# A two-layer hybrid encoder on one core: the order of the instructions on TensorE, VectorE and ScalarE, written out anew

## The chip, the core and the metric

The kernel runs on one core of a Trainium2 chip. The metric is device time in microseconds (us) for one execution. Work goes to five engines, each with its own instruction row that it runs strictly from front to back: TensorE (PE in the profile; PEld is its loading of the stationary operand), VectorE (DVE), ScalarE (ACT), GpSimd (POOL) and SyncE (SP), which issues the weight DMAs here. Engines wait for each other by semaphores. An instruction that waits holds up everything behind it in its own row.

## What is computed

Two layers on a sequence of 256 tokens of width 1024. Cut to what matters:

```python
for i in range(2):
    proj = x @ w_in[i]                       # 1024 -> 13824, split into ten parts
    y_a = multiscale_pool(a_in) @ w_branch_a[i]
    y_b = dilated_attention(q, k, v) @ w_branch_b[i]      # 12 heads, three dilations
    y_c = hgrn2_bidirectional(q_h, i_h, f_fwd, f_bwd, g_h) @ w_branch_c[i]   # 8 heads
    merged = gates[0] * y_a + gates[1] * y_b + gates[2] * y_c
    x1 = layer_norm(ALPHA * x + merged @ w_out[i])
    hidden = silu(x1 @ w_ffn_gate[i]) * (x1 @ w_ffn_up[i])
    ple = (p[i] @ w_ple_proj[i]) * sigmoid(x1 @ w_ple_gate[i])
    x = layer_norm(ALPHA * x1 + hidden @ w_ffn_down[i] + ple)
```

All is float32. The recurrence of branch C is computed without a loop over tokens: running products of the forget gate (scans) and their reciprocals turn it into small matrix products per block of 64 tokens.

## The kernel before

**Chunks.** All weights stream through as chunks of 1 MB (`raw`, by SyncE, L197), three buffers deep. A chunk is split into two reduced-precision parts: ScalarE copies it to `whi` (L210), VectorE subtracts to get `wlo` (L211). TensorE then makes three products per tile (L252 to L254: hi by hi, hi by lo, lo by hi); the FFN's first half uses two wider ones (L272). A chunk is 48 products with 256 moving columns or 24 with 512. Activations are split alike, into `xx`.

```python
PE.matmul(ps, lhsT=ah, rhs=bh, start=first, stop=False)    # L252
PE.matmul(ps, lhsT=ah, rhs=bl, start=False, stop=False)    # L253
PE.matmul(ps, lhsT=al, rhs=bh, start=False, stop=last)     # L254
```

**A layer in order.** V of branch C (4 chunks), its output gate (4), then four head pairs, each with three chunks (query, forward and backward forget gate) and, for the first three, two chunks of the attention's V; twelve chunks of attention queries and keys; four of pooling; the three branches with their gates; the output projection and norm 1; the per-layer embedding (`pl2`); 22 chunks of FFN gate and up; 11 of FFN down and norm 2.

**Background tasks.** What branch C, attention and pooling do between their chunks are Python generators (`hgrn_task`, `attn_task`, `pool_task`). After each chunk `step_end` splits the next chunk and then runs `background`, which resumes a task until about 3000 estimated ns are handed out. A `yield None` puts a task to sleep until the next chunk. For a head pair and direction, `hgrn_task` puts on VectorE: two scans (L388/L390 or L393/L396), two reciprocals (L401, L403), four products (L405 to L409), one copy, eight small products (L431, L433), one tiny product (L437) and two more (L441). On TensorE follow 8 block products (L451) and, after the second direction, 8 more (L461) and 4 (L468); later the products with V (L492, L493) and transposes (L517). Attention's transposes are L553.

**The norms.** `rows_gemm` fills four PSUM banks (two token halves t, two column halves) and holds the last two or three chunks, so that the half t=0 is complete first. `layer_norm` then adds the residual (L341/L343), takes statistics (L344 to L348), has GpSimd raise to the power -0.5 (L320), corrects that on VectorE (L322 to L325), scales in two steps (L353, L355), and TensorE transposes the result (L330) so that the next stage can use it (split by L311 and L312).

**What sets the order.** Only the opening stretch (first chunks and transposes of `x`) runs in the order in which it is written. After that the programming layer's scheduler places the instructions on each engine by its own estimates.

Of the kernel before, what the change touches and what calls it, by code (L numbers as in the profile page):

```python
# [15 lines left out]
P = 128  # L16
# [62 lines left out]
def trunk(ctx: ExitStack, tc: tile.TileContext, x, p, w_in, pool_w, pool_scale, w_branch_a,  # L79
# [4 lines left out]

    cst = ctx.enter_context(tc.tile_pool(name="cst", bufs=1))
# [36 lines left out]
    def load_x(t):  # L122
        for hf in range(2):
            cs = slice(512 * hf, 512 * hf + 512)
            nc.sync.dma_start(out=xt[:, t, cs], in_=x[0, t * P:(t + 1) * P, cs])
# [13 lines left out]
    for l in range(DEPTH):  # L139
        for c0 in (C_IH, C_IH + 512, C_GH, C_GH + 512):  # L140
            blk(w_in[l], 0, c0)
            blk(w_in[l], 512, c0)
        for hp in range(4):
            for c0 in (C_QH, C_FF, C_FB):
                cols(w_in[l], c0 + 256 * hp)
            if hp < 3:
                blk(w_in[l], 0, C_VA + 512 * hp)
                blk(w_in[l], 512, C_VA + 512 * hp)
# [37 lines left out]
    def pieces(i, k):  # L186
        n = {0: 4, 1: 2}.get(i, 1)
        return [slice(j * k // n, (j + 1) * k // n) for j in range(n)]

    def dma_chunk():  # L190
        i = pos["dma"]
        if i >= NCH:
            return
        src, k = chunks[i]
        t = wp.tile([P, k, 2048 // k], F32, tag="raw", name="raw")
        for ks in pieces(i, k):
            nc.sync.dma_start(out=t[:, ks, :], in_=src[:, ks, :])  # L197
        raw[i] = t
        pos["dma"] += 1

    def split_chunk():
        i = pos["split"]
        if i >= NCH:
            return
        k = chunks[i][1]
        t = raw.pop(i)
        hi = wp.tile([P, k, 2048 // k], F32R, tag="whi", name="whi")
        lo = wp.tile([P, k, 2048 // k], F32R, tag="wlo", name="wlo")
        for ks in pieces(i, k):
            A.activation(out=hi[:, ks, :], in_=t[:, ks, :], func=AF.Copy)  # L210
            V.tensor_tensor(out=lo[:, ks, :], in0=t[:, ks, :], in1=f(hi[:, ks, :]), op=ALU.subtract)  # L211
        split[i] = (hi, lo)
        pos["split"] += 1
        dma_chunk()
# [6 lines left out]

    tasks = []
    busy = []

    def background(budget=3000, width=3):
        slept = set()
        while budget > 0:
            act = [t for t in tasks[:width] if id(t) not in slept]
            if not act:
                return  # L230
            t = act[0]
            try:
                c = next(t[1])
                if c is None:
                    slept.add(id(t))
                else:
                    budget -= c
            except StopIteration:
                tasks.remove(t)

    def finish(kind):
        while any(t[0] == kind for t in tasks):
            background(10 ** 9)

    def step_end():
        split_chunk()
        background()
# [8 lines left out]
    def gemm_cols(w, act, ps, nk=8, m0=0, nm=2):  # L256
        for m in range(nm):
            for k in range(nk):
# [31 lines left out]
    def gemm_tok(ws, act, evac, between):  # L290

        nk = 4 * len(ws)
        for t in range(2):
            ps = gbank()
            for k in range(nk):
                w = ws[k // 4]
                mm3(ps, act(k, t), (w[0][:, k % 4, :], w[1][:, k % 4, :]), k == 0, k == nk - 1)
                if t == 0 and k == 5 and between is not None:
                    between()
            evac(t, ps)  # L300

    def tok_block(act, evac, between=None, n=2):
        ws = [use_chunk() for _ in range(n)]
        gemm_tok(ws, act, evac, between)
        for _ in range(n):
            step_end()
# [11 lines left out]
    def rsqrt(out, v, n):  # L318
        y = small([P, n], "rs_y")
        G.tensor_tensor(out=y, in0=v, in1=mhalf.to_broadcast([P, n]) if n > 1 else mhalf, op=ALU.pow)  # L320
# [6 lines left out]
    def transpose_x(t, hf):  # L327
        ps = tbank()
        for k in range(4):
            PE.transpose(ps[:, k * P:(k + 1) * P], xt[:, t, (4 * hf + k) * P:(4 * hf + k + 1) * P], ident)  # L330
        v = ps.rearrange("p (k t) -> p k t", t=P)
        split_to(xh[:, 4 * hf:4 * hf + 4, t * P:(t + 1) * P],
                 xl[:, 4 * hf:4 * hf + 4, t * P:(t + 1) * P], v)

    def layer_norm(t, gb, ress, then):

        st = small([P, 2, 6], "ln_st")
        for hf, (base, scale, ps) in enumerate(ress):
            dst = xt[:, t, 512 * hf:512 * hf + 512]
            if scale is None:  # L340
                V.tensor_tensor(out=dst, in0=base, in1=ps, op=ALU.add)  # L341
            else:
                V.scalar_tensor_tensor(out=dst, in0=base, scalar=scale, in1=ps, op0=ALU.mult, op1=ALU.add)  # L343
            V.bn_stats(out=st[:, hf, :], in_=dst)  # L344
        mv = small([P, 2], "ln_mv")
        V.bn_aggr(out=mv, in_=st)
        ve = small([P, 1], "ln_ve")
        V.tensor_scalar(out=ve, in0=mv[:, 1:2], scalar1=LN_EPS, scalar2=None, op0=ALU.add)  # L348
        r = small([P, 1], "ln_r")
        rsqrt(r, ve, 1)  # L350
        for hf in range(2):
            cs = slice(512 * hf, 512 * hf + 512)
            V.scalar_tensor_tensor(out=xt[:, t, cs], in0=xt[:, t, cs], scalar=mv[:, 0:1], in1=gb[:, 0, cs],  # L353
                                   op0=ALU.subtract, op1=ALU.mult)
            V.scalar_tensor_tensor(out=xt[:, t, cs], in0=xt[:, t, cs], scalar=r, in1=gb[:, 1, cs],  # L355
                                   op0=ALU.mult, op1=ALU.add)
            then(t, hf)
# [8 lines left out]
    def hgrn_task(l, hp, q, ff, kf, fb, kb, vt, gt, oh, ol):  # L366
# [14 lines left out]
        for d in range(2):  # L381
# [63 lines left out]
            if dg is None:  # L445
                dg = tbank()
            for h in range(2):
# [24 lines left out]
            yield None  # L472
# [11 lines left out]
        A.activation(out=al, in_=lg.rearrange("p (g c) -> p g c", c=P), func=AF.Copy)  # L484
        yield 660
        yield None
        po = tbank()
# [6 lines left out]
        yield None  # L494
# [7 lines left out]
        rsqrt(r, ms, 4)  # L502
        yield 700
        yield None
        for t in range(2):
# [5 lines left out]
            yield 400  # L511
        yield None
        pt = tbank()
# [4 lines left out]
        yield None  # L518
        for h in range(2):
# [3 lines left out]
            yield 330  # L523


    def attn_task(j, qs, ks, va, vb, ob):
        hh = j % 2
        sj = slope(j)
        po = None
        for t in range(2):  # L530
# [5 lines left out]
            yield None  # L536
# [7 lines left out]
            A.activation(out=sc, in_=sc, func=AF.Exp, bias=nm, accum_out=den)  # L544
            yield 900
            rd = small([P, 1], "rd")
            V.reciprocal(out=rd, in_=den)
            V.tensor_scalar(out=sc, in0=sc, scalar1=rd, scalar2=None, op0=ALU.mult)
            yield 500
            yield None  # L550
            pp = tbank()
# [4 lines left out]
            yield None  # L556
            if po is None:
                po = tbank()
            o = po[:, t * P:(t + 1) * P]
            js = slice(j * P, (j + 1) * P)  # L560
# [4 lines left out]
        yield None  # L565
# [5 lines left out]
        yield 330  # L571


    def pool_task(g, a, mix):

        while busy or any(t[0] == "attn1" for t in tasks):
            yield None
# [26 lines left out]
        yield 850  # L604
        mh, ml = half2k([P, 2, S], F32R), half2k([P, 2, S], F32R)
        split_to(mh, ml, a[:, :, 8:264])
        mix[g] = (mh, ml)
# [5 lines left out]
    load_x(0)  # L613
    dma_chunk()
    dma_chunk()
    load_x(1)
    dma_chunk()
    start = ctx.enter_context(ExitStack())
    start.enter_context(tc.manual_schedule(engines={
        mybir.EngineType.Activation, mybir.EngineType.DVE, mybir.EngineType.PE}))  # L620
    for hf in range(2):
        transpose_x(0, hf)
    split_chunk()
    split_chunk()
    def begin():
        for hf in range(2):
            transpose_x(1, hf)
        split_chunk()

# [35 lines left out]
    for l in range(DEPTH):  # L665
# [3 lines left out]
        for hf in range(2):  # L669
            def ev(t, ps):  # L670
                A.activation(out=vt[:, t, 512 * hf:512 * hf + 512], in_=ps, func=AF.Copy)
            tok_block(xtok, ev, begin if l == 0 and hf == 0 else None)
            if l == 0 and hf == 0:
                start.close()
            if l == 0 and hf == 1:
                load_constants()
        for hf in range(2):
            def ev(t, ps):
                s = misc([P, 512])
# [280 lines left out]
```

## Time and profile before

| | |
|---|---|
| median of 3 runs | 1318.82 us (1318.72 to 1318.83) |
| the profiled execution | 1319.02 us; from its first to its last instruction 1317.2 us |
| granted TensorE clock, mean | 0.997 |
| TensorE busy / weight load | 1292.2 us / 1140.0 us |
| VectorE / ScalarE / GpSimd busy | 900.2 / 617.4 / 20.0 us |
| moved by DMA | 233.36 MB, mean 177 GB/s |

Busy times of TensorE are unions of pipelined, overlapping instructions; what a product costs is read from the distance between the starts of two. In a row of the timeline stand the start, the duration, engine, line, operation, output<-inputs, shape, how many in a row, and in brackets how long the engine had been idle before and what released it. Lines are those of the kernel before (L252) unless the changed kernel is named.

### The profile page before, as it was taken

How to read it: one execution, taken by the hardware profiler on the slowest of the kernel's cores; microseconds unless marked ns; L12 is line 12 of the kernel's file. 1: busy time of each engine (PE TensorE's matmuls, PEld its weight loads, DVE VectorE, ACT ScalarE, POOL GpSimd, SP SyncE). 2: the span in 40 equal slices, each digit the busy share in tenths (PEclk: the TensorE clock that was granted, in tenths of full speed). 3: DMA queues.
4: the chain of work that ended last, by engine and by line, in shares of the span. 5: the costliest groups of instructions: out<-in, count | busy, mean ns of one | idle time of the engine just before them, and what ended most of it. 6: DMA issues, size and time to landing. Idle time of an engine off the chain costs nothing.

```text
span 1317.2 us, 18830 instructions
## 1 busy us (share of the span) xinstructions
PE 1292.2 (98%) x7881; PEld 1140.0 (87%) x7881; DVE 900.2 (68%) x1230; ACT 617.4 (47%) x732; POOL 20.0 (2%) x24
## 2 busy tenths in 40 slices
PE   8999999999999999999989999999999999999997
PEld 6899999998888788888779999999988887888885
DVE  4697998575656776664555989975846658666645
ACT  5444445444444455553344444445534444555531
POOL 0000000000000000000000000000000000000000
PEclk9999999999999999999999999999999999999999
DMA  8655444244656466655356545453355664766550
GB/s 301 206 183 170 160 160 161 97 158 157 197 199 223 161 224 192 191 188 197 128 176 208 169 152 170 152 181 107 128 192 192 198 226 140 243 192 189 187 197 34
DMA packets 160276, 233.36 MB, mean 177 GB/s; under 512 B 3840, under 2 KB 108864, under 8 KB 160192
## 3 DMA queue, kind: packets, MB, share of 16 engines
q1 hardware_dynamic: 158496, 227.44, 52.4%
q10 hardware_dynamic: 1696, 4.72, 1.1%
q8 instruction: 62, 1.02, 0.3%
q14 instruction: 22, 0.18, 0.0%
HBM read 231.10 MB, written 1.05 MB: 176 GB/s over the span
## 4 chain that ended last, share of the span: by engine, by line
PE 91%; DVE 6%; ACT 1%; issue 1%; POOL 1%; DMA 0%; POOLq 0%; SPq 0%; DVEq 0%; ACTq 0%
PE g L252 22%; PE g L253 22%; PE g L254 22%; PE t L272 9%; PE g L272 9%; DVE wlo L211 2%; ACT whi L210 1%; PE t L451 1%; POOL rs_y L320 1%; PE t L492 1%; PE t L493 1%; PE t L468 0%; PE t L330 0%; DVE ln_st L344 0%; PE t L533 0%
## 5 line engine op out<-in xcount | busy, mean ns | idle before, releaser
L211 DVE TENSOR_TENSOR wlo<-raw,whi 128x2048 fp32r<-128x2048 f32 (+2 forms) x218 | 490.1, 2249 | 305.7 <-ACT whi L210 305.3
L210 ACT ACTIVATE whi<-raw 128x2048 fp32r<-128x2048 f32 (+2 forms) x218 | 410.1, 1883 | 368.5 <-PE g L254 191.6
L252 PE MATMUL g<-xx,whi 128*128 128x256 f32 x896 | 256.9, 287 | 0.0
L253 PE MATMUL g<-xx,whi 128*128 128x256 f32 x896 | 253.9, 283 | 0.0
L254 PE MATMUL g<-xx,wlo 128*128 128x256 f32 x896 | 253.7, 283 | 0.0
L252 PE MATMUL g<-whi,xx 128*128 128x512 f32 x480 | 189.5, 395 | 1.7 <-ACT whi L210 1.6
L253 PE MATMUL g<-wlo,xx 128*128 128x512 f32 x480 | 189.2, 394 | 1.4 <-DVE wlo L211 1.4
L254 PE MATMUL g<-whi,xx 128*128 128x512 f32 x480 | 188.0, 393 | 0.0
L252 PEld LDWEIGHTS g<-xx,whi 128*128 128x128 f32 x896 | 171.7, 192 | 0.7
L253 PEld LDWEIGHTS g<-xx,whi 128*128 128x128 f32 x896 | 171.8, 192 | 0.2
L254 PEld LDWEIGHTS g<-xx,wlo 128*128 128x128 f32 x896 | 171.6, 192 | 0.0
L272 PE MATMUL t<-xx,whi 128*128 128x512 f32 x352 | 123.6, 396 | 0.0
L272 PE MATMUL g<-xx,whi 128*128 128x512 f32 x352 | 123.6, 396 | 0.0
L252 PEld LDWEIGHTS g<-whi,xx 128*128 128x128 f32 x480 | 91.6, 191 | 21.5 <-ACT whi L210 2.2
L253 PEld LDWEIGHTS g<-wlo,xx 128*128 128x128 f32 x480 | 91.6, 191 | 21.0 <-DVE wlo L211 2.6
L254 PEld LDWEIGHTS g<-whi,xx 128*128 128x128 f32 x480 | 91.3, 190 | 18.9
L272 PE MATMUL g<-xx,wlo 128*128 128x256 f32 x352 | 90.9, 279 | 0.0
L272 PE MATMUL t<-xx,wlo 128*128 128x256 f32 x352 | 90.9, 279 | 0.0
L253 PE MATMUL g<-wlo,s 128*128 128x512 f32 x224 | 87.5, 391 | 0.0
L254 PE MATMUL g<-whi,s 128*128 128x512 f32 x224 | 87.5, 390 | 0.0
L252 PE MATMUL g<-whi,s 128*128 128x512 f32 x224 | 87.1, 390 | 0.0
L272 PEld LDWEIGHTS g<-xx,whi 128*128 128x128 f32 x352 | 64.5, 188 | 12.0
(181 smaller groups left out, 1662.5 us busy)
## 6 DMA issues: line engine op xcount, KB each, us to landing
raw<-in_w_in_dram SPq DMA_DIRECT2D x106, 1024.0 KB, 5.1
raw<-in_w_ffn_gate_dram SPq DMA_DIRECT2D x22, 1024.0 KB, 5.3
raw<-in_w_ffn_up_dram SPq DMA_DIRECT2D x22, 1024.0 KB, 5.4
raw<-in_w_ffn_down_dram SPq DMA_DIRECT2D x22, 1024.0 KB, 4.9
raw<-in_w_branch_c_dram SPq DMA_DIRECT2D x8, 1024.0 KB, 5.1
raw<-in_w_branch_a_dram SPq DMA_DIRECT2D x8, 1024.0 KB, 5.0
raw<-in_w_out_dram SPq DMA_DIRECT2D x8, 1024.0 KB, 5.3
raw<-in_w_ple_gate_dram SPq DMA_DIRECT2D x8, 1024.0 KB, 5.1
```

Source lines behind the costliest of these rows:

```text
L210: A.activation(out=hi[:, ks, :], in_=t[:, ks, :], func=AF.Copy)
L211: V.tensor_tensor(out=lo[:, ks, :], in0=t[:, ks, :], in1=f(hi[:, ks, :]), op=ALU.subtract)
L252: PE.matmul(ps, lhsT=ah, rhs=bh, start=first, stop=False)
L253: PE.matmul(ps, lhsT=ah, rhs=bl, start=False, stop=False)
L254: PE.matmul(ps, lhsT=al, rhs=bh, start=False, stop=last)
L272: PE.matmul(o, lhsT=a, rhs=b, start=k == 0 and i == 0, stop=k == KD - 1 and i == 1, skip_group_check=True)
L320: G.tensor_tensor(out=y, in0=v, in1=mhalf.to_broadcast([P, n]) if n > 1 else mhalf, op=ALU.pow)
L451: PE.matmul(dg[po:po + 64, co:co + 64], lhsT=KI[:, cs], rhs=QI[:, cs], start=True, stop=True)
L492: PE.matmul(o, lhsT=at[:, 2 * h + t, :], rhs=vt[:, t, hs], start=True, stop=False)
L493: PE.matmul(o, lhsT=al[:, 2 * h + 1 - t, :], rhs=vt[:, 1 - t, hs], start=False, stop=True)
```

## The change

The whole kernel now keeps TensorE, VectorE and ScalarE in the order in which the code is written (`manual_schedule` at its start). The code is rewritten for that:

- `step_end` runs the background first, then a stage's evacuation, then the split of the next chunk. A new `amid` stands in the middle of each chunk's products and wakes sleeping tasks there, so that a task's TensorE part stands amid a chunk's products. `background` takes tasks in turn.
- Banks and 2 KB buffers are counted by hand (`banks_for`, `room`). Before a stage takes a buffer of which ten are held, `room` runs background tasks until one is free. Two head pairs' tasks hold ten.
- The output gate's four chunks (G) move from before the head pairs to behind the first pair's three; the attention's V follows one pair later. Pooling's weight chunk moves behind branch B.
- A norm becomes class `Norm` (`add`, `rest`) and the step after it class `Handover`: the half t=0 is normalised while TensorE finishes t=1; t=1's norm stands ahead of the splits of the next two chunks on VectorE (`split_later` gives their ScalarE half first); the next stage begins with products that need only t=0 and only `whi`.
- The head: `x` and the first two chunks are loaded and split in smaller pieces, in the order of their use, and four products on zeros (`spin`) run on TensorE before and after the first transposes.

The counts of products and other operations are the same but for the four `spin` products, one memset and some splits cut in pieces. In the diff, `go`'s arguments are the token half, the column half, the chunk and which of the three products; `a` and `b` of `Handover` are the two chunks still held. The diff, cut to its core:

```diff
+    ctx.enter_context(tc.manual_schedule(engines={
+        mybir.EngineType.Activation, mybir.EngineType.DVE, mybir.EngineType.PE}))
...
+    def amid(width=3):
+        for t in tasks[:width]:
+            if id(t) in asleep:
+                asleep.discard(id(t))
+                resume(t)
     def background(budget=3000, width=3):
-        slept = set()
+        turn = 0
         while budget > 0:
-            act = [t for t in tasks[:width] if id(t) not in slept]
+            act = [t for t in tasks[:width] if id(t) not in asleep]
             if not act:
                 return
-            t = act[0]
...
+            t = act[turn % len(act)]
+            turn += 1
+            budget -= resume(t) or 0
+    def room(n):
+        while held[0] + n > 10:
+            amid()
+            background(1000)
+        held[0] += n
-    def step_end():
-        split_chunk()
-        background()
+    def step_end(then=None):
+        background()
+        if then is not None:
+            then()
+        split_chunk()
...
     def gemm_cols(w, act, ps, nk=8, m0=0, nm=2):
         for m in range(nm):
+            if m == 1:
+                amid()
...
             for i in range(6):
                 ps = gbank()
                 gemm_cols(use_chunk(), xk, ps)
+                room(1)
                 t = half2k([P, 512])
...
+        class Handover:
+            def __init__(self, norms, banks, part, a, b):
+                norms[0].rest()
+                part(*a, 1, 0)
+                part(*b, 1, 0)
+                norms[1].add(0, banks[1][0])
+                part(*a, 1, 1)
+                part(*b, 1, 1, (0,))
+                split_x(0, 0, turn_x(0, 0))
+                part(*b, 1, 1, (1,))
+                split_x(0, 1, turn_x(0, 1))
+                norms[1].add(1, banks[1][1])
+                norms[1].rest()
+                self.lo = [split_later() for _ in range(2)]
...
+            go(0, 0, 0, (0, 2))
+            go(0, 0, 0, (1,))
+            go(0, 0, 1, (0, 1))
+            go(0, 1, 0, (0, 1))
+            norm1.finish()
+            norm1.lo[0]()
+            norm1.finish_lo()
+            norm1.lo[1]()
+            go(1, 0, 0, (0, 2))
+            go(0, 0, 1, (2,))
...
+            idle = tbank()
+            spin(3)
+            ps = [gbank(), gbank()]
+            first = turn_x(0, 0)
+            spin(1)
+            split_x(0, 0, first)
```

**Norm 2 of layer 0, on VectorE.** Before, from the last scaling of t=0 to the end of t=1's statistics (x is the residual, g a PSUM bank, xx the split activations, s_5340 the norm's gain and bias):

```order
L355 SCALAR_TENSOR_TENSOR x<-x,ln_r,s_5340 128x512 x2
L341 TENSOR_TENSOR x<-x,g 128x512
L312 TENSOR_TENSOR xx<-t,xx 128x4x128
L344 BN_STATS ln_st<-x 128x6
L312 TENSOR_TENSOR xx<-t,xx 128x4x128
L211 TENSOR_TENSOR wlo<-raw,whi 128x2048
L341 TENSOR_TENSOR x<-x,g 128x512
L211 TENSOR_TENSOR wlo<-raw,whi 128x2048
L344 BN_STATS ln_st<-x 128x6
L211 TENSOR_TENSOR wlo<-raw,whi 128x2048
L346 BN_AGGR ln_mv<-ln_st 128x2
```

Of the changed kernel, the second half of t=1's norm (L432 is the old L341, L435 the old L344, L447 and L452 the old L353 and L355, L215 the old L211, L417 the old L312):

```order
L432 TENSOR_TENSOR x<-x,g 128x512
L435 BN_STATS ln_st<-x 128x6
L440 BN_AGGR ln_mv<-ln_st 128x2
L442 TENSOR_SCALAR ln_ve<-ln_mv 128x1
L447 SCALAR_TENSOR_TENSOR x<-x,ln_mv,s_5351 128x512 x2
L395 TENSOR_TENSOR rs_t<-rs_y 128x1
L396 TENSOR_TENSOR rs_t<-rs_t,ln_ve 128x1
L397 TENSOR_SCALAR rs_t<-rs_t 128x1
L398 TENSOR_TENSOR ln_r<-rs_t,rs_y 128x1
L452 SCALAR_TENSOR_TENSOR x<-x,ln_r,s_5351 128x512 x2
L215 TENSOR_TENSOR wlo<-raw,whi 128x2048
L417 TENSOR_TENSOR xx<-t,xx 128x4x128 x2
```

Three splits of weights stood inside t=1's norm; now they stand behind it.

**The third head pair's second direction, on VectorE, and TensorE's block products that use it.** Before, VectorE from the last small products to the next pair's scan, with two splits between (w are the pair's buffers; TensorE's L451 of this direction comes amid the products of a later chunk, of attention queries and keys):

```order
L431 TENSOR_TENSOR w<-h,w 128x3x32
L433 TENSOR_TENSOR w<-w,tot 128x3x32
L441 TENSOR_TENSOR w<-w,t_1800 128x2x64 x2
L388 SCALAR_TENSOR_TENSOR w<-kc,h 128x512
L211 TENSOR_TENSOR wlo<-raw,whi 128x2048
L414 COPY tot<-w 128x16
L437 TENSOR_TENSOR t_2046<-tot 128x8
L211 TENSOR_TENSOR wlo<-raw,whi 128x2048
```

In the changed kernel, VectorE's rows of this direction run from the split behind the fourth pair's forward-gate chunk to the `room` call after the first attention query chunk (L491 and L494 are its scans, L499 and L501 its reciprocals, L503 to L507 the old L405 to L409, L900 an edge of the forget gate):

```order
L215 TENSOR_TENSOR wlo<-raw,whi 128x2048
L491 SCALAR_TENSOR_TENSOR w<-kc,h 128x512
L494 SCALAR_TENSOR_TENSOR w<-h,kc 128x512
L499 RECIPROCAL w<-w 128x8x32
L501 RECIPROCAL w<-w 128x8x32
L900 TENSOR_SCALAR h<-h 128x2
L215 TENSOR_TENSOR wlo<-raw,whi 128x2048
L503 TENSOR_TENSOR w<-h,w 128x8x32
L504 TENSOR_TENSOR w<-h,w 128x8x32
L506 TENSOR_TENSOR w<-h,w 128x8x32
L507 TENSOR_TENSOR w<-h,w 128x8x32
L512 COPY tot<-w 128x16
```

On TensorE the block products (L552, L562 and L569 are the old L451, L461 and L468) stand right behind that chunk's 48 products, whose first ones and last ones are L320 to L322, the old L252 to L254:

```order
L320 MATMUL g<-xx,whi 128x256
L321 MATMUL g<-xx,whi 128x256
L322 MATMUL g<-xx,wlo 128x256
L552 MATMUL t<-w 64x64 x8
L562 MATMUL t<-w 64x64 x8
L569 MATMUL t<-w 128x128 x4
L320 MATMUL g<-xx,whi 128x256
```

Before, two splits and the next pair's scan separated VectorE's last product from TensorE's use of it; now VectorE's products and TensorE's use are written in the same pass, at the end of the chunk.

**The head, on TensorE.** Before, eight transposes and then products of t=0 alone:

```order
L330 MATMUL t<-ident,x 128x128 x8
L252 MATMUL g<-whi,xx 128x512
L253 MATMUL g<-wlo,xx 128x512
L254 MATMUL g<-whi,xx 128x512
L252 MATMUL g<-whi,xx 128x512
```

Now (L805 are the products on zeros, L408 transposes, L369 products of a chunk):

```order
L805 MATMUL t<-w 128x256 x3
L408 MATMUL t<-ident,x 128x128 x4
L805 MATMUL t<-w 128x256
L369 MATMUL g<-whi,xx 128x512 x2
L369 MATMUL g<-wlo,xx 128x512
L369 MATMUL g<-whi,xx 128x512 x2
L369 MATMUL g<-wlo,xx 128x512
L408 MATMUL t<-ident,x 128x128 x4
```

Products on zeros are added, and the transposes are spread between the products of the first chunk, which now serves both token halves in turn.

More of the change, by code (lines that the diff above doesn't have):

```diff
@@ L120, in trunk, with load_x @@
     xt = slot("x", [P, 2, D])
[L122 to L125, printed above, removed]
+    def load_x(t, hf):
+        cs = slice(512 * hf, 512 * hf + 512)
+        nc.sync.dma_start(out=xt[:, t, cs], in_=x[0, t * P:(t + 1) * P, cs])
     chunks = []
@@ L204, in split_chunk, with split_later @@
             return
[L205 to L214, printed above, removed]
+        k, hi_part, lo_part = split_begin()
+        hi_part(slice(0, k))
+        lo_part(slice(0, k))
+    def split_later():
+        k, hi_part, lo_part = split_begin()
+        hi_part(slice(0, k))
+        return lambda: lo_part(slice(0, k))
     def use_chunk():
@@ L325, in rsqrt, with turn_x @@
         V.tensor_tensor(out=out, in0=t, in1=y, op=ALU.mult)
-    def transpose_x(t, hf):
+    def rsqrt(out, v, n):
+        y = small([P, n], "rs_y")
+        G.tensor_tensor(out=y, in0=v, in1=mhalf.to_broadcast([P, n]) if n > 1 else mhalf, op=ALU.pow)
+        newton(out, y, v, n)
+    def turn_x(t, hf):
         ps = tbank()
@@ L330, in transpose_x, with split_x @@
             PE.transpose(ps[:, k * P:(k + 1) * P], xt[:, t, (4 * hf + k) * P:(4 * hf + k + 1) * P], ident)
+        return ps
+    def split_x(t, hf, ps, hi=True, lo=True):
         v = ps.rearrange("p (k t) -> p k t", t=P)
[L332 to L341, printed above, removed]
-            else:
[L343 to L357, printed above, removed]
@@ L484, in hgrn_task @@
         A.activation(out=al, in_=lg.rearrange("p (g c) -> p g c", c=P), func=AF.Copy)
+        free(3)
         yield 660
         yield None
+        while l not in gated:
+            yield None
+        yield from banks_for(1)
         po = tbank()
@@ L570, in attn_task, with pool_task @@
         split_to(nat(ob[:, 0, j, :]), nat(ob[:, 1, j, :]), src)
-        yield 330
-    def pool_task(g, a, mix):
-        while busy or any(t[0] == "attn1" for t in tasks):
+        free(1)
+        yield 400
+    def pool_task(l, g, a, mix):
+        while busy or scored[0] < 4 * l + 4:
             yield None
@@ L668, in trunk, with ev @@
         gt = slot("s5", [P, 2, D])
[L669 to L679, printed above, removed]
-                A.activation(out=s, in_=ps, func=AF.Sigmoid)
-                V.tensor_tensor(out=gt[:, t, 512 * hf:512 * hf + 512], in0=ps, in1=s, op=ALU.mult)
-            tok_block(xtok, ev)
+        def ev(hf, t, ps):
+            A.activation(out=vt[:, t, 512 * hf:512 * hf + 512], in_=ps, func=AF.Copy)
@@ L777, in trunk @@
         finish("attn1")
+        for n in range(2):
+            branch(n, slot("s7", [P, 2, 512]), tok_of(lambda k: ob[:, 0, k, :], lambda k: ob[:, 1, k, :]), pieces=1)
+        pT = slot("s7", [P, 2, S])
+        nc.scalar.dma_start(out=pT, in_=p[l, 0].rearrange("(t p) c -> p t c", p=P))
         finish("pool")
@@ L812, in turn_later @@
             turn(n)
-            yield 2000
+            yield 1300
         for n in range(2):
@@ L925, in hact @@
             return a[:, 0, k % 4, tk], a[:, 1, k % 4, tk]
-        rows_gemm(NF // 2, 3, hact, ln2)
+        norms = [Norm(t, gb, None) for t in range(2)]
+        if not last:
+            norm1 = Handover(norms, *rows_gemm(NF // 2, hact, norms))
+        else:
+            banks, part, a, b = rows_gemm(NF // 2, hact, norms)
+            norms[0].rest(store)
+            for hf in range(2):
+                part(*a, 1, hf)
+                part(*b, 1, hf)
+                norms[1].add(hf, banks[1][hf])
+            norms[1].rest(store)
 _INS = ['x', 'p', 'w_in', 'pool_w', 'pool_scale', 'w_branch_a', 'w_branch_b', 'w_branch_c',
```

491 lines of the change are left out of this document (339 added, 152 removed).

## The prediction

> **What bounds the kernel now.** I began with the page's busy times, which name the engine.
>
> ```profile
> PE 1292.2 (98%) x7881; PEld 1140.0 (87%) x7881; DVE 900.2 (68%) x1230; ACT 617.4 (47%) x732; POOL 20.0 (2%) x24
> ```
>
> TensorE is the bound, and its products stay as they are. An order can win only what lies between them, so next came TensorE's waits.
>
> ```profile
> PE t L330 <- DVE x L355: 7.8, 6, 3.5
> PE t L330 <- DMA x<-in_x_dram: 3.5, 1, 3.5
> PE g L252 <- ACT whi L210: 1.6, 1, 1.6
> PE g L253 <- DVE wlo L211: 1.4, 1, 1.4
> PE t L553 <- DVE s L509: 1.3, 2, 0.7
> PE t L492 <- DVE m L483: 0.4, 2, 0.2
> ```
>
> All of TensorE's waits of any size are here: 7.8 + 1.4 = 9.2 us at the norms, 3.5 + 1.6 at the start, 1.3 + 0.4 in the background. The longest stands behind norm 2 of layer 0; the timeline shows TensorE first, then VectorE, then the stretches on both sides (columns: length, TensorE's busy time and instructions, ..., granted clock, DMA share, GB/s).
>
> ```profile
> 667.76 1.75 PE L330 MATMUL t<-ident,x 128*128 128x128 f32 x8 [3.54 <-DVE x L355]
> ...
> 661.87 2.28 DVE L211 TENSOR_TENSOR wlo<-raw,whi 128x2048 fp32r<-128x2048 f32 x1
> 666.87 1.42 DVE L355 SCALAR_TENSOR_TENSOR x<-x,ln_r,s 128x512 f32<-128x512 f32 x2
> ...
> 664.20:667.70 3.50, 0.02 (x1) 0.00 (x0) 2.93 (x10) 0.60 (x1) 0.92 (x1) 1.00 1.03 377
> 668.20:671.60 3.40, 3.40 (x12) 2.69 (x11) 1.47 (x3) 1.20 (x2) 0.00 (x0) 0.50 0.13 48
> ```
>
> Weight splits like the one at 661.87 delay the norm, whose last scaling starts at 666.87; TensorE idles 3.54 us, and the next 3.4 us run at clock 0.50: half of that, 1.7 us, is lost besides. TensorE's 1.4 us wait, in the row of L253 above, was followed by no such stretch.
>
> The prices of VectorE, ScalarE and the switch on TensorE come from the third and fourth head pairs. The first column gives start-to-start distances, which I use where VectorE works without a break.
>
> ```profile
> 77.03 2.29 DVE L211 TENSOR_TENSOR wlo<-raw,whi 128x2048 fp32r<-128x2048 f32 x1
> 79.22 0.42 DVE L405 TENSOR_TENSOR w<-h,w 128x256 f32<-128x256 f32 x1
> 79.56 0.42 DVE L408 TENSOR_TENSOR w<-h,w 128x256 f32<-128x256 f32 x1
> 80.31 0.26 DVE L431 TENSOR_TENSOR w<-h,w 128x96 f32<-128x96 f32 x1
> 81.66 0.17 DVE L437 TENSOR_TENSOR t<-tot 128x8 f32<-128x8 f32 x1
> 81.74 1.23 DVE L393 TENSOR_TENSOR_SCAN w<-kc,h 128x512 f32<-128x512 f32 x1
> 82.87 0.48 DVE L441 TENSOR_TENSOR w<-w,t 128x128 f32<-128x128 f32 x2
> 84.71 1.76 DVE L401 RECIPROCAL w<-w 128x256 f32<-128x256 f32 x1
> 86.37 4.44 DVE L211 TENSOR_TENSOR wlo<-raw,whi 128x2048 fp32r<-128x2048 f32 x2
> ...
> 103.64 0.58 ACT L698 ACTIVATE h<-g 128x512 f32<-128x512 f32 x1
> 104.12 0.59 ACT L701 ACTIVATE h<-g 128x512 f32<-128x512 f32 x1
> 110.32 1.92 ACT L210 ACTIVATE whi<-raw 128x2048 fp32r<-128x2048 f32 x1 [2.20 <-PE g L254]
> ...
> 89.46 0.12 PE g L254
> 89.58 0.62 PE t L451 x16
> 90.19 0.32 PE g L252
> ...
> 178.13 0.49 DVE L441 TENSOR_TENSOR w<-w,t 128x128 f32<-128x128 f32 x2
> ...
> 186.81 0.69 PE L451 MATMUL t<-w 128*64 128x64 f32 x16
> ```
>
> A split costs VectorE 79.22 - 77.03 = 2.19 us, a product 0.34, a scan 1.13, a reciprocal 86.37 - 84.71 = 1.66, eight small products 1.35. A chunk is 48 x 0.12 = 5.76 us. The last two rows show the cover of before: VectorE was done 8.2 us ahead of TensorE's use.
>
> **The change part by part.** *Norms.* The three splits leave the way. From the last product of a token half VectorE needs the chain that the tail shows, where nothing else is in its row:
>
> ```profile
> 1308.69 0.69 DVE L341 TENSOR_TENSOR x<-x,g 128x512 f32<-128x512 f32 x1 [1.17 <-PE g L254]
> ...
> 1311.63 0.16 DVE L322 TENSOR_TENSOR rs_t<-rs_y 128x1 f32<-128x1 f32 x1 [0.44 <-POOL rs_y L320]
> 1311.71 0.75 DVE L353 SCALAR_TENSOR_TENSOR x<-x,ln_mv,s 128x512 f32<-128x512 f32 x1
> ...
> 1312.94 1.41 DVE L355 SCALAR_TENSOR_TENSOR x<-x,ln_r,s 128x512 f32<-128x512 f32 x2
> ```
>
> That is 4.25 us to the last scaling and 0.7 to its first half. Both L353 now stand ahead of L322: the second fills the 0.44 us of waiting for GpSimd, so 0.4 goes, and a normalised first half takes 4.55 us, 4.64 with the semaphores. Meanwhile TensorE has 20 products of t=1 (23 with the last three): 20 x 0.23 = 4.6 us. Its transposes meet their input with 0.1 us of idling. For t=1 VectorE, after t=0's last activation split at about 7.9, needs 4.55: ready at 12.5. TensorE has two groups of four transposes (0.4 each), 3 products, and 28 products of the next stage, 0.8 + 0.7 + 6.4, and comes at about 12.6. With 0.3 us where the first products of t=1 wait for their split, some 0.45 us of idling is left at norm 2 of layer 0 and 0.15 at each norm 1: 0.75 in all. Gain 9.2 - 0.75 = 8.45, and 1.7 for the slow stretch: **-10.15** (between -5, if half the overlap holds, and -10.9). The splits that moved behind the norm end at about 15.3 and 18.6, and are wanted at 16.0 and 20.6.
>
> *Background waits.* The 1.3 + 0.4 us of L553 and L492 go, since their tasks are spread further: **-1.7** (bounds 0 and -1.7).
>
> *Fewer switches.* Small exact products are now gathered in 63 places on TensorE instead of 71. By the rows at 89.46 a switch back costs 0.32 - 0.12 = 0.20: 8 x 0.2 = **-1.6** (bounds 0 and, if both directions cost as much, -3.2).
>
> *The head.* The start has two things to win, the wait of 1.6 us and products at half pace.
>
> ```profile
> 7.36 0.79 PE L252 MATMUL g<-whi,xx 128*128 128x512 f32 x1 [1.61 <-ACT whi L210]
> 9.10 0.63 PE L252 MATMUL g<-whi,xx 128*128 128x512 f32 x1
> 9.53 0.63 PE L253 MATMUL g<-wlo,xx 128*128 128x512 f32 x1
> ...
> 13.14 0.40 PE L253 MATMUL g<-wlo,xx 128*128 128x512 f32 x1
> 13.37 0.40 PE L254 MATMUL g<-whi,xx 128*128 128x512 f32 x1
> ```
>
> The first twelve products come 0.43 us apart, later ones 0.23: 12 x 0.2 = 2.4 us. The four products on zeros run while TensorE would idle and cost nothing. Together 4.0 us are to be had, but ScalarE must make its pieces (0.6 us each) of `x` and of two chunks in a row before TensorE is free of it. Adding these up I get half: **-2.0** (bounds -4.0, and +1 if the pieces' fixed costs win). [...]
>
> *The tail.* Its norm gains the 0.4 us worked out above: **-0.4** (0 to -0.7).
>
> *What is put on the path.* At the first attention query chunk `room` needs a buffer that only the third pair's second direction frees. So this direction's products stand on TensorE right behind that chunk, and VectorE reaches them late. Zero is the end of the fourth pair's forward-gate products. ScalarE's evacuation takes 0.2 + 0.48 + 0.47, the next `whi` 1.92: VectorE's split begins at 3.1. Then, in the order shown, split 2.19, two scans 2.26, two reciprocals 3.27 (1.66 and 1.61), split 2.19, four products 1.36, edge and semaphore 0.1: done at 14.47. TensorE has the backward-gate chunk 5.76, one background insertion 0.62 + 0.20 and the query chunk 5.76: it arrives at 12.34 and idles 2.1 us. Its L552 takes 0.62 us; of VectorE's copy, eight small products, L437 and L441, 0.08 + 1.35 + 0.08 + 0.4 = 1.9 us, TensorE's L552 and L562 (0.5 us) cover 1.0, and 0.9 more is waited for: 3.0 us in layer 0. Layer 1 has gate operations more per chunk:
>
> ```profile
> L705 DVE TENSOR_SCALAR h<-h,omlb,lb 128x256 f32<-128x256 f32 x16 | 6.0, 417 | 0.0
> L707 DVE TENSOR_SCALAR h<-h,omlb 128x256 f32<-128x256 f32 x16 | 5.7, 354 | 0.0
> ```
>
> Two of each stand ahead of the split: 2 x (0.33 + 0.25) = 1.16 us (the durations less the overlap of 0.09), so 4.2. Together **+7.2** (bounds 0, if VectorE is 2 us ahead of my sum, and +12, if it is 2.4 us behind in both layers). The first piece in layer 1 is 3.3 us long, nearest to the 3.54 that was followed by half clock; that in layer 0, 2.1, is nearest to the 1.4 that was not: **+1.7** once (0 to 3.4).
>
> Elsewhere the same adding leaves every use of the background 0.8 to 1.6 us of slack at five places a layer, more at the others; SP's weight transfers keep their order and three buffers, and stay ahead.
>
> Sum: -10.15 - 1.7 - 1.6 - 2.0 - 0.4 + 7.2 + 1.7 = -6.95 on the profiled execution's 1319.0, so 1312.05. The median of the runs is 0.2 lower: **1312**.
>
> **The rivals.** *No gap at `room`.* If VectorE runs 2 to 3 us ahead of my sum there, the 7.2 and 1.7 fall away: 1312 - 8.9 = 1303. For it: it waits nowhere long in the rows at 77 to 91. Against: its rows up to the third pair's last product are fixed by the order, and each was priced without a pause.
>
> *Half the overlap.* If VectorE's operations end later than I count (their durations are 0.09 longer than their distances), each norm's chain is 1.2 us longer and the splits come late: half of 10.15 stays, 1312 + 5.1 = 1317.
>
> *The other sign: VectorE is late everywhere.* In a fixed order one late engine delays all behind it. If VectorE's lag at the insertions is about 2 us more than by my adding, the five tight places of both layers lose about 0.7 each, 7 us, and both `room` places 2 us each, 4 more: 1312 + 11 = 1323. It decides from a lag of 1.3 us on. Against: after each insertion VectorE has a chunk of 5.76 us for 2.19 of splitting, and catches up.
>
> *No slow stretch at `room`.* A gap of 3.3 us is shorter than the 3.54 that had one; then 1312 - 1.7 = 1310.3. [...]
>
> **How the numbers follow.** Forecast (1308 to 1316): 0.47. No slow stretch, inside the same range: 0.08. No gap: 0.15. Half the overlap: 0.13. VectorE late: 0.10. The rest, 0.07, lies about evenly. A change within 0.2%, 2.6 us, can't be told from none by a measurement of this kernel: faster ends at 1316.2, slower begins at 1321.4. Faster: 0.47 + 0.08 + 0.15 = 0.70; same: 0.13 + 0.05 of the rest; slower: 0.10 + 0.02. The range reaches from 1302.5, just under the case without a gap, to 1320, over that with half the overlap; late VectorE stays outside.
>
> **What would show it.** Right: L408 (the old L330) waits under 1 us in all at the norms, no clock of 0.50 behind norm 2, TensorE's L552, L562 and L569 wait some 3 and 4 us for VectorE right behind the first query chunk of each layer, first products under 6.5 us. Wrong: no idling at that place; norm waits above 4 us; new waits over 0.5 us at several insertions; or weight DMAs among TensorE's releasers.

## The result: slower by 1.8%, and the profile after

The changed kernel takes 1341.77 us (median of 4 runs, 1341.55 to 1342.19), the kernel before 1318.77 us beside it (1318.17 to 1318.83): ratio 1.0176 with a 95% interval of 1.0158 to 1.0193. Forecast were 1312 us and a range up to 1320. The profiled run has a span of 1339.6 us against 1317.2, so 22.4 us are to be explained.

TensorE's waits in the changed kernel (total us, times and the longest; s is pool's output, w a head pair's buffers). From here on the lines are those of the changed kernel, where nothing else is said: L320 to L322 and L369 are products, L390 and L215 VectorE's splits of activations and of weights, L801 the memset of the zeros.

```profile
PE t L320 <- DVE s L390: 14.3, 8, 3.9
PE t L552 <- DVE w L507: 5.7, 2, 3.5
PE t L805 <- DVE w L801: 1.5, 1, 1.5
PE g L321 <- DVE wlo L215: 0.8, 2, 0.4
PE g L369 <- ACT whi L212: 0.8, 2, 0.5
PE t L562 <- DVE w L531: 0.6, 2, 0.3
PE g L369 <- ACT xx L415: 0.2, 1, 0.2
```

The norms' row (7.8 us for L330 before) is gone, and L552, which the forecast named, is there. The first row, the longest, was in no term of the forecast. The line is a product of pool's weight chunk. The rows show its first occurrence in layer 0: TensorE, then VectorE, then stretches of time with the clock (the column before the last two).

```profile
368.53 0.29 PE L322 MATMUL t<-h,wlo 128*128 128x256 f32 x1
372.72 0.58 PE L320 MATMUL t<-h,whi 128*128 128x256 f32 x1 [3.90 <-DVE s L390]
376.73 0.58 PE L320 MATMUL t<-h,whi 128*128 128x256 f32 x1 [1.08 <-DVE s L390]
380.75 0.58 PE L320 MATMUL t<-h,whi 128*128 128x256 f32 x1 [1.08 <-DVE s L390]
...
369.38 0.69 DVE L981 TENSOR_TENSOR s<-s,s 128x512 f32<-128x512 f32 x1
369.99 2.28 DVE L215 TENSOR_TENSOR wlo<-raw,whi 128x2048 fp32r<-128x2048 f32 x1
372.19 0.47 DVE L390 SCALAR_TENSOR_TENSOR s<-t,vec,s 128x256 fp32r<-128x256 f32 x1
...
368.00:371.50 3.50, 0.82 (x7) 0.60 (x5) 3.43 (x5) 2.30 (x2) 0.00 (x0) 1.00 0.79 255
371.50:374.90 3.40, 2.18 (x10) 2.18 (x11) 1.17 (x2) 0.47 (x1) 0.00 (x0) 0.50 0.77 220
374.90:378.30 3.40, 2.32 (x11) 2.02 (x11) 0.97 (x2) 0.47 (x1) 0.00 (x0) 0.50 0.57 216
381.70:385.10 3.40, 2.32 (x11) 2.02 (x10) 0.97 (x2) 0.95 (x2) 0.00 (x0) 0.50 0.00 0
385.20:388.60 3.40, 3.40 (x12) 2.92 (x12) 0.48 (x1) 2.15 (x2) 0.00 (x0) 0.50 0.00 0
388.60:392.00 3.40, 3.40 (x16) 2.77 (x16) 2.29 (x1) 0.12 (x1) 0.00 (x0) 1.00 0.00 0
```

TensorE makes six products, the first half of a PSUM bank, and then waits 3.9 us before the second half of the same bank. What releases it is VectorE's split of the first half (L390), and VectorE still has the end of branch B's evacuation (L981, 0.69 us) and a 2.28 us weight split (L215) in front. From 371.5 to 388.6 the clock is at 0.50, five stretches of 3.4 us. In the first four TensorE is busy for 2.2 to 2.3 us, with an idle of 1.08 us at each group; behind the first stretch without an idle the clock is 1.00 again. Adding up all distances above the normal 0.228 and 0.12 us, this chunk loses 4.07 + 9.56 us in layer 0 and 4.07 + 9.77 in layer 1, 27.5 together.

The kernel before has the same chunk, written the same way, one branch earlier, and its TensorE doesn't wait. These are its rows:

```profile
336.96 0.28 PE L253 MATMUL t<-h,whi 128*128 128x256 f32 x1
337.08 0.28 PE L254 MATMUL t<-h,wlo 128*128 128x256 f32 x1
337.20 0.40 PE L252 MATMUL g<-whi,xx 128*128 128x512 f32 x1
...
339.27 0.39 PE L252 MATMUL g<-whi,xx 128*128 128x512 f32 x1
339.50 0.28 PE L252 MATMUL t<-h,whi 128*128 128x256 f32 x1
...
336.60 2.28 DVE L211 TENSOR_TENSOR wlo<-raw,whi 128x2048 fp32r<-128x2048 f32 x1
338.80 1.66 DVE L315 SCALAR_TENSOR_TENSOR s<-t,vec,s 128x256 fp32r<-128x256 f32 x4
```

The scheduler had put the first halves of all four groups in a row (24 products, up to 337.20), ten products of the next chunk behind them, and then the second halves from 339.50 on; VectorE's splits, here too behind a weight split, start at 338.80 and are still in time. The written order, kept word for word now, has first half, split, second half for one group after the other.

The second row of the waits is the `room` place that the forecast spoke of: first layer 0, with the clock, then layer 1.

```profile
175.94 0.69 PE L552 MATMUL t<-w 128*64 128x64 f32 x16 [2.19 <-DVE w L507]
177.03 1.12 PE L562 MATMUL t<-w 128*64 128x64 f32 x14 [0.30 <-DVE w L531]
...
173.50:176.90 3.40, 1.05 (x21) 0.70 (x19) 3.40 (x13) 0.00 (x0) 0.00 (x0) 1.00 0.31 95
177.00:180.40 3.40, 3.37 (x25) 3.25 (x26) 3.37 (x9) 0.96 (x3) 0.00 (x0) 0.50 0.59 203
...
837.53 0.69 PE L552 MATMUL t<-w 128*64 128x64 f32 x16 [3.50 <-DVE w L507]
```

### The profile page after: what moved, and what is told of

It is laid out like the page before. It is cut to its first block, busy times and chain, and to the rows that moved or that the text cites. A ratio compares the mean times of both kernels' runs of the same rounds, so it can differ in the third digit from the quotient of the medians.

```text
span 1339.6 us, 18867 instructions
## 1 busy us (share of the span) xinstructions
PE 1305.8 (97%) x7889; PEld 1152.9 (86%) x7889; DVE 907.6 (68%) x1233; ACT 615.0 (46%) x734; POOL 16.7 (1%) x24
## 3 DMA queue, kind: packets, MB, share of 16 engines
HBM read 231.10 MB, written 1.05 MB: 173 GB/s over the span
## 4 chain that ended last, share of the span: by engine, by line
PE 74%; DVE 12%; ACT 8%; issue 5%; ACTq 0%; DVEq 0%
PE g L369 32%; PE g L320 11%; PE g L321 11%; PE g L322 11%; ACT whi L212 7%; DVE wlo L215 6%; DVE m L349 2%; DVE m L1163 1%; PE g L342 1%; PE t L569 1%; PE t L320 1%; PE t L552 1%; PE t L645 1%; PE t L408 1%; PE t L598 1%
## 5 line engine op out<-in xcount | busy, mean ns | idle before, releaser
L215 DVE TENSOR_TENSOR wlo<-raw,whi 128x2048 fp32r<-128x2048 f32 (+1 forms) x220 | 489.4, 2229 | 315.3 <-ACT whi L212 315.2
L212 ACT ACTIVATE whi<-raw 128x2048 fp32r<-128x2048 f32 (+1 forms) x220 | 409.2, 1864 | 178.3 <-PE g L369 107.3
L369 PE MATMUL g<-whi,xx 128*128 128x512 f32 x960 | 295.9, 395 | 1.1 <-ACT whi L212 0.8
L320 PE MATMUL g<-xx,whi 128*128 128x256 f32 x896 | 256.8, 287 | 0.0
L321 PE MATMUL g<-xx,whi 128*128 128x256 f32 x896 | 253.9, 283 | 0.0
L322 PE MATMUL g<-xx,wlo 128*128 128x256 f32 x896 | 253.7, 283 | 0.0
L369 PEld LDWEIGHTS g<-whi,xx 128*128 128x128 f32 x960 | 180.3, 191 | 38.0 <-ACT whi L212 2.2
L369 PE MATMUL g<-wlo,xx 128*128 128x512 f32 x480 | 182.7, 393 | 0.2
L320 PEld LDWEIGHTS g<-xx,whi 128*128 128x128 f32 x896 | 172.3, 192 | 0.7
L321 PEld LDWEIGHTS g<-xx,whi 128*128 128x128 f32 x896 | 172.3, 192 | 0.3
L322 PEld LDWEIGHTS g<-xx,wlo 128*128 128x128 f32 x896 | 172.2, 192 | 0.0
L369 PEld LDWEIGHTS g<-wlo,xx 128*128 128x128 f32 x480 | 91.3, 190 | 20.9 <-DVE wlo L215 1.8
L342 PEld LDWEIGHTS t<-xx,whi 128*128 128x128 f32 x352 | 64.5, 188 | 11.9
L342 PEld LDWEIGHTS t<-xx,wlo 128*128 128x128 f32 x352 | 66.4, 189 | 3.9
L342 PEld LDWEIGHTS g<-xx,wlo 128*128 128x128 f32 x352 | 66.4, 189 | 3.9
L369 PE MATMUL g<-whi,s 128*128 128x512 f32 x192 | 59.1, 389 | 0.0
L320 PE MATMUL g<-whi,s 128*128 128x512 f32 x128 | 50.1, 392 | 0.0
```

The source lines that it names most:

```text
L342: PE.matmul(o, lhsT=a, rhs=b, start=k == 0 and i == 0, stop=k == KD - 1 and i == 1, skip_group_check=True)
L369: PE.matmul(ps, lhsT=a, rhs=b, start=i == 0 and k == 0 and p == 0, stop=i == n - 1 and k == 3 and p == 2)
```

## The experiments

Theory after the result ("halves"): the order of the halves of a bank makes TensorE wait for VectorE; the long idle brings the clock to half, the short ones keep it there. Rivals: the *place* of the chunk, behind branch B, where VectorE is later; and a half *clock* with another cause. All times are medians with the ratio to the kernel before from the same chip.

| kernel | us | ratio, 95% interval |
|---|---|---|
| halves in turn | 1318.96 | 1.0000 (0.9991 to 1.0010) |
| halves apart | 1313.99 | 0.9966 (0.9954 to 0.9978) |
| first idle filled | 1329.93 | 1.0085 (1.0070 to 1.0100) |
| other idles filled | 1334.74 | 1.0123 (1.0108 to 1.0138) |
| pool's chunk in its old place | 1336.41 | 1.0127 (1.0110 to 1.0144) |
| `room` one chunk later | 1341.52 | 1.0174 (1.0159 to 1.0189) |
| splits ahead of the norm | 1359.57 | 1.0313 (1.0293 to 1.0333) |
| halves apart, V blocks spread | 1306.12 | 0.9907 (0.9890 to 0.9923) |
| the same, three chunks held at the end | 1306.63 | 0.9911 (0.9896 to 0.9926) |
| the same with V spread, no products on zeros | 1306.72 | 0.9914 (0.9899 to 0.9928) |

**Halves in turn.** First halves of all groups, then all second halves:

```diff
-        for g in range(4):
-            ps = tbank()
-            mh, ml = mix[g]
-            for m in range(2):
+        pb = [tbank() for _ in range(4)]
+        for m in range(2):
+            for g in range(4):
+                ps = pb[g]
+                mh, ml = mix[g]
```

> Pool's weight chunk in the changed kernel with the first halves of all four groups ahead of the second halves (24 products, then 24), nothing else. Theory 'halves': TensorE waits because the second half of a bank comes right behind the first, whose split stands on VectorE behind the branch's evacuation and a weight split; the 3.9 us of idling then bring the clock to 0.50, and three more idles of 1.1 us keep it there for 17 us. Then 18 more products lie ahead of the first wait: idle 3.9 - 18 x 0.12 = 1.7 to 1.9 us per layer, no clock of 0.50 there, 1341.8 - 27.5 + 3.8 = 1318 us. Rival 'place': VectorE is too late at this place in any order, one stretch of half clock stays in each layer: about 1325 to 1328. Rival 'clock': the 17 us at half clock have another cause and stay: about 1331.

Measured: 1318.96. The wait falls from 14.3 us in eight to 3.6 in two:

```profile
PE t L320 <- DVE s L390: 3.6, 2, 1.8
...
368.40:371.80 3.40, 2.63 (x23) 2.43 (x21) 3.37 (x4) 2.65 (x5) 0.00 (x0) 1.00 0.91 297
371.80:375.20 3.40, 2.39 (x20) 2.39 (x21) 2.77 (x7) 1.39 (x4) 0.00 (x0) 1.00 0.72 209
...
1020.30:1023.70 3.40, 1.62 (x14) 1.48 (x13) 3.04 (x5) 1.77 (x5) 0.00 (x0) 1.00 0.85 242
1023.80:1027.20 3.40, 3.40 (x16) 3.21 (x16) 1.56 (x4) 1.62 (x4) 0.00 (x0) 0.50 0.73 275
```

The size is as expected. One thing isn't: the same idle of 1.78 us is followed by a stretch at 0.50 in layer 1 (1023.80) and not in layer 0. The stretches in the rows are laid so that they end where the clock's own record of this run changes, in steps of 3.413 us counted back from the change between 1023.70 and 1023.80. So laid, layer 0's idle falls into two of them (TensorE busy for 2.63 and 2.39 us of 3.40), layer 1's into one (1.62).

**Halves apart.** As above, and twelve products of the next gate chunk between them:

```diff
+            if m == 0:
+                ahead = (use_chunk(), gbank(), gbank())
+                tok_part(ahead[1], ahead[0], 0, 2, xtok, 0)
```

> As with the halves in turn, and twelve products of the next gate chunk (token half 0) between first and second halves, as the kernel before has ten there. 'Halves': no idling in the pool chunk, no half clock there, both losses of 13.6 and 13.8 us gone: 1314 us, which is the time forecast within 2 us. 'Place': VectorE's first split at this place still ends later than 36 products allow in both layers, a wait above 1 us is left: 1317 or more. 'Clock': 1331.

Measured: 1313.99; no wait of L320 on L390 is left, and no half clock at the chunk. The whole loss of 27.5 us at the chunk was its order: in the same place, with another order, it is gone.

**First idle filled.** In the changed kernel, 17 needless products behind the first half of the first group:

```diff
+                if m == 0:
+                    fill(17 if g == 0 else 0)
```

> The changed kernel with 17 needless products of 512 columns (17 x 0.228 = 3.9 us, into a free bank, their result unused) behind the first half of the first group: they fill the long idle, all other waits stay. If the long idle brings the half clock, no clock of 0.50 follows at the pool chunk; 3.9 of products and three idles of about 1.1 us are left per layer: 1314.3 + 2 x 7.2 = 1329 us. If idles of 1.1 us in 2.5 bring it just as well, or if it has its own cause, the 17 us stay: 1341 to 1342.

Measured: 1329.93. The other waits are all there, and the clock stays at 1.00:

```profile
PE t L320 <- DVE s L390: 6.5, 6, 1.1
...
374.50:377.90 3.40, 1.69 (x12) 1.49 (x12) 1.37 (x4) 1.18 (x3) 0.00 (x0) 1.00 0.63 240
```

So the idle of 3.9 us brings the half clock here; the idles of 1.1 us alone, with TensorE busy for 1.69 of 3.40 us in the emptiest stretch shown, don't.

**Other idles filled.** `fill(0 if g == 0 else 5)` instead:

> The changed kernel with five needless products of 512 columns behind the first half of each of the other three groups of the pool chunk, and none behind the first group: the idle of 3.9 us stays, the three of 1.1 us are filled. If the half clock lasts 17 us because each following stretch of 3.4 us has an idle of 1.1 us in it, one full stretch ends it: one stretch of 3.4 us at 0.50 per layer instead of five, and the loss per layer is 4.1 + 1.7 + 3 x 5 x 0.228 = 9.2 instead of 13.7 us: 1314 + 18.4 = 1332 us. If its length has nothing to do with the idles, five stretches stay and the time is 1341 to 1343.

Measured: 1334.74, with two stretches at half clock per layer instead of five:

```profile
366.60:370.00 3.40, 0.94 (x8) 0.69 (x6) 3.33 (x5) 2.39 (x2) 0.00 (x0) 1.00 0.72 248
370.10:373.50 3.40, 2.05 (x9) 2.05 (x10) 1.30 (x2) 0.36 (x1) 0.00 (x0) 0.50 0.67 207
373.50:376.90 3.40, 3.40 (x13) 2.92 (x12) 0.97 (x2) 0.59 (x2) 0.00 (x0) 0.51 0.62 234
376.90:380.20 3.30, 3.30 (x24) 2.81 (x23) 0.97 (x2) 0.95 (x2) 0.00 (x0) 1.00 0.00 0
```

I had expected one: the long idle reaches into the first stretch (busy 2.05), and only the second is full. The short idles of 1.08 us do prolong the half clock, from 6.8 to 17.07 us. The same run holds a counterexample at `room` in layer 0: the idle is 2.19 us as in the changed kernel, but the clock stays at 1.00 (see the last section).

**Old place.** Pool's chunk ahead of branch B again, halves as written (the weight order and the loop are moved, nothing else).

> The changed kernel with pool's weight chunk back ahead of branch B, where the kernel before has it, its halves in the written order as in the changed kernel. Theory 'halves': the written order of the halves makes TensorE wait here too. VectorE has one evacuation operation per token half less in front than behind branch B (2 x 0.67 us), so the first wait is some 2.5 us instead of 3.9, the three of 1.1 stay; with five stretches at half clock again 1339, without them 1314 + 2 x 5.8 = 1326. Rival 'place': in this place VectorE is early enough, the waits go, 1314 us.

Measured: 1336.41, and the wait is back to what it was behind branch B:

```profile
PE t L320 <- DVE s L390: 14.1, 8, 3.8
...
337.55 2.29 DVE L215 TENSOR_TENSOR wlo<-raw,whi 128x2048 fp32r<-128x2048 f32 x1 [1.03 <-ACT whi L212]
339.76 0.48 DVE L390 SCALAR_TENSOR_TENSOR s<-t,vec,s 128x256 fp32r<-128x256 f32 x1
```

The place falls as a rival: with the written order both places lose the time, with the halves apart neither does (behind branch B in the run above, ahead of it in the kernel before). My 2.5 us for the first wait was wrong: the weight split in front starts when ScalarE's half is done, so one evacuation less on VectorE makes nothing earlier. This kernel's five runs lie between 1333.56 and 1341.82 us, with mean clocks of 0.990 to 0.982: the share of the time at half clock differed among them.

**`room` one chunk later.** The first query chunk's evacuation waits for the second's:

```diff
+                if jp == 0 and i == 0:
+                    ps0 = ps
+                    step_end()
+                    continue
+                room(2 if jp == 0 and i == 1 else 1)
```

> The changed kernel with the first attention query chunk's room and evacuation put off by one chunk (its result stays in its PSUM bank), so that TensorE's L552 to L569 of the third pair's second direction stand one chunk later. Theory 'room': VectorE has 5.76 us more for one more split of 2.19, so the waits of 3.5 us at most there vanish, and the stretch of 3.4 us at half clock behind them in both layers: 1341.8 - (5.1 + 6.4 - 1.0) = 1331.3 us. Rival: the wait only moves on, to the next insertion or to L552 of the fourth pair: 1338 to 1342.

Measured: 1341.52, no gain.

```profile
PE t L552 <- DVE w L507: 5.3, 2, 2.8
...
210.19 0.69 PE L552 MATMUL t<-w 128*64 128x64 f32 x16 [2.47 <-DVE w L507]
```

The wait at 173 us is gone, but one of 2.47 us stands at 210.19, at the fourth pair's second direction: the rival was right. A second one, of 2.78 us, stands there in layer 1. VectorE isn't late at one place; it lags through this stage. In the changed kernel it is busy for 64.08 of 72 us around there (behind the length stand busy time and count of TensorE, its weight load, VectorE, ScalarE and GpSimd):

```profile
120.00:192.00 72.00, 69.51 (x577) 66.61 (x576) 64.08 (x113) 31.89 (x50) 2.02 (x2) 0.98 0.47 154
```

**V blocks spread.** Therefore, with the halves apart, chunks that ask little of VectorE come between the fourth pair and the query chunk:

```diff
-            for g in {1: (0, 1), 2: (2,)}.get(hp, ()):
+            for g in {1: (0,), 2: (1,), 3: (2,)}.get(hp, ()):
```

> The kernel with the pool chunk's halves apart (1314.0), and of the attention V's three blocks of two chunks one stands behind each of the second, third and fourth head pair, instead of two behind the second and one behind the third. VectorE is 89% busy around the fourth pair; the two chunks now between that pair and the first attention query chunk give it 2 x (5.5 - 2.2) = 6.6 us for 2.2 to 3.5 us of lateness. Theory 'room': both waits of L552 and both stretches at half clock go, 1314 - 10.5 = 1303.5 us, up to 1308 if the room now wanted at the fourth pair is waited for. Rival 'VectorE is short over the whole stage': its lateness turns up at the fourth pair instead, 1312 to 1318.

Measured: 1306.12. Its waits are:

```profile
PE t L598 <- DVE m L585: 1.7, 1, 1.7
PE t L806 <- DVE w L802: 1.5, 1, 1.5
PE g L321 <- DVE wlo L215: 0.9, 2, 0.4
PE g L369 <- ACT whi L212: 0.9, 2, 0.5
PE g L369 <- ACT xx L416: 0.2, 1, 0.2
...
120.00:192.00 72.00, 72.00 (x569) 67.11 (x564) 66.88 (x120) 34.02 (x52) 2.03 (x2) 1.00 0.48 156
```

L552 (here L553) waits no more, no stretch at half clock is left before the end, and VectorE has done more in the same 72 us. Of the 10.5 us expected, 7.9 came; 1.7 turned into a wait in layer 1 (L598). This kernel is the fastest of all, 0.9% under the kernel before.

**Splits ahead of the norm.** In the changed kernel's `Handover`:

```diff
+                self.lo = [split_later() for _ in range(2)]
+                for lo in self.lo:
+                    lo()
                 norms[1].add(1, banks[1][1])
                 norms[1].rest()
```

> The changed kernel with VectorE's two weight splits put back ahead of the end of t=1's norm at the three norms between stages, nothing else. If that norm is on the path (as the forecast has it, with 0.1 us to spare), 2 x 2.19 us more make TensorE's transposes of t=1 wait about 4 us at each, and half clock for 3.4 us after some: 3 x 4.2 + up to 3 x 1.7 = 12 to 17 us more, 1354 to 1359. If the splits were not what cost the kernel before its idling there: 1342.

Measured: 1359.57, 17.8 us more than the changed kernel, a little over the 12 to 17 expected.

```profile
PE t L408 <- DVE x L452: 11.9, 3, 5.2
```

A wait per norm, and 6.8 us at half clock behind each, 3.4 more than expected. So splits ahead of t=1's norm do make TensorE idle there; that they were all of the kernel before's idling, which had three splits among the norm's operations, is argued from this and not shown.

**Tail.** Three chunks held at the end of layer 1:

> As with the V blocks spread, and the last stage of layer 1 holds three chunks instead of two, so that t=0 is complete 2.7 us earlier and its norm is off VectorE before TensorE ends. The changed kernel's VectorE goes from t=0's norm straight to both columns of t=1, 1.3 us later than TensorE allows; that goes: 1.2 us less than the kernel with the V blocks spread. Rival: nothing, since the last chunk's arrival sets the end.

Measured: 1306.63, no gain. TensorE's last product starts 8.74 us before the end instead of 9.79, close to the 1.2 us expected, but a new wait of 1.4 us for the split of the last held chunk eats it:

```profile
PE g L321 <- DVE wlo L215: 2.3, 3, 1.4
```

**No products on zeros.**

> The kernel with the pool chunk's halves apart and the V blocks spread (1306.1), without the four products on zeros at the start. If they bring the clock up before the first products, the first dozen products come at 0.43 instead of 0.23 us: up to 12 x 0.2 = 2.4 us more, 1307 to 1308.5. If not, the time stays at 1306.1 or falls a little.

Measured: 1306.72, 0.6 us more than with them and under the 1307 to 1308.5 expected; the kernel before beside it was 0.4 us faster. In the traces the 96th product of 512 columns (four chunks' worth) starts at 32.22 us instead of 31.62, 0.6 us later too. Here two products of 512 columns together take 1.03 us or more up to the pair at 10.82 us, and 0.63 at 11.97; in the changed kernel, with the products on zeros, pairs take 0.62 to 0.73 from the first, at 6.44 us, on. That the products on zeros help is likely; by how much stays open, with one trace of this kernel.

## Why the prediction was wrong

The step that failed is the sentence "Elsewhere the same adding leaves every use of the background 0.8 to 1.6 us of slack at five places a layer, more at the others". It covered the hand-made insertions, but pool's own weight chunk, whose move the description of the change names, got no term, and the cover that hid its splits before, 24 products and ten more of another chunk, was not named. The row at 338.80 of the kernel before against the written order would have shown it: VectorE's first split ends some 4 us after TensorE's sixth product. These 27.5 us are most of the miss of 29.8: with the pool chunk put right alone the kernel takes 1313.99 us, 2 us above the forecast. That nearness is in part luck, since the steps below miss in both directions.

Every sign of being right came true: no wait of L408 at the norms, no half clock behind norm 2, waits of L552 and L562 of 2.5 and 3.8 us at `room`, the first product at 6.44 us. None of them concerned pool's chunk. The rival with the other sign, VectorE late everywhere, came nearest in time (1323), but not by its mechanism: L552 waits at the two `room` places and at no other insertion.

By steps, for the profiled runs:

- *Norms*, forecast -10.15: the 7.8 and 1.4 us of waits and the 1.7 of half clock are gone but for 0.2 (L369 on L415), -10.7. The mechanism is confirmed by the splits ahead of the norm.
- *Background waits*, -1.7: gone, as forecast. New are two waits of L321 for a weight split early in FFN down (0.41 us at 619.16, 0.43 at 1281.14): +0.8.
- *Head*, -2.0: the 96th product of 512 columns starts at 31.48 instead of 32.78 us, -1.3. The four products on zeros are eight records, most of them 0.43 us apart, 3.4 us, and the first chunk's products behind them come 0.23 us apart, so the slow pace did not stay.
- *Tail*, -0.4: became +0.8 (the last product starts 9.78 us before the end, before 8.97). VectorE's norm of t=0 now runs into t=1's end, which the forecast, pricing t=1's chain alone, missed.
- *`room`*, +7.2 and +1.7: the first waits were 2.19 and 3.50 us where 2.1 and 3.3 stood. In total 5.11 and 6.56 us were lost by distances above 0.12 us for 256 columns, less 0.73 each that the same insertion costs at 86.49 and 212.04, where nothing waits: +10.2. The half clock came in both layers, not only behind the longer wait. That it needs an idle near 3.5 us was wrong: 2.19 us, and once 1.78, were enough.
- *Pool's chunk*, no term: +27.5.

These come to -10.7 - 1.7 + 0.8 - 1.3 + 0.8 + 10.2 + 27.5 = +25.6; measured are +22.4. The remainder, -3.2, is what the eight switches fewer (forecast -1.6) and small things can have brought; it was not measured alone.

The rival without a slow stretch at `room` is wrong. Idles shorter than the 3.54 us of the kernel before were followed by half clock: 2.19 us (a stretch with 1.05 us of TensorE's work, 173.50) and 1.78 us (1.62, at 1020.30 with the halves in turn). As for the return, stretches in which TensorE was busy for 2.2 to 2.3 of 3.4 us at half clock (371.50 to 385.10) did not bring it back, the first full one did (3.40 from 385.20, clock 1.00 from 388.60).

## What to carry to other kernels

When a kernel goes from a scheduler's order to the written one, walk every place where an engine reads a result and another writes beside it (two halves of one bank, whose order cost 27.5 us here), not only the places that the change was made for: list what the scheduler had put between, since that is the cover. In a stage where VectorE was busy for 64.08 of 72 us, moving a wait of 2.19 us by one chunk only moved it on (2.47 us at 210.19); chunks that ask less of that engine, put in between, removed it. And price an idle of TensorE with what follows: here 3.9 us of waiting cost 13.7, with short idles behind it that kept the clock down (five stretches at half clock, two with these idles filled).

## What the runs showed of the hardware

Up to TensorE's last products, half clock came in stretches of 3.41 us or of a whole number of them: 3.41 and 17.07 us in the changed kernel, 6.8 with the other idles filled. In the changed kernel their starts lie a whole number of 3.413 us apart (176.956, 371.516, 839.142 and 1033.702 us: 57, 137 and 57 steps). Equal idles had different outcomes. With the halves in turn, the idle of 1.78 us was followed by half clock in one layer, where it lay in one step (busy 1.62), and not in the other, where it lay across two (2.63 and 2.39). The 2.19 us at `room` in layer 0 were followed by it in the changed kernel, where they lay in one step (1.01 of 3.41, from 173.54), and not with the other idles filled, where they lay across two (which meet at 175.50). That alone doesn't settle it: in the old place they lay across two as well (at 174.90), and half clock followed.

How much work in a step is enough isn't shown. With the steps laid to end where the clock changes, these two rows of the `room` place contradict any single bound: the first (other idles filled) was not followed by half clock, the second (old place), with more work in it, was.

```profile
172.10:175.50 3.40, 1.58 (x14) 1.37 (x12) 3.40 (x7) 0.00 (x0) 0.00 (x0) 1.00 0.00 0
174.90:178.30 3.40, 1.88 (x35) 1.66 (x36) 3.37 (x17) 0.27 (x1) 0.00 (x0) 1.00 0.70 229
```

No run moved an idle by itself. In the changed kernel full clock came back behind steps in which TensorE was busy for 3.34 us (from 176.96), 3.40 (from 839.15) and 3.41 (from 385.17 and from 1047.36), not behind those of 2.18 to 2.32 (371.50 to 385.10).
